# Casting a head's keys and queries in two halves, with another draw of the instruction order and 151 moves behind it

## The chip, the cores and the metric

The kernel runs on one core of one Trainium2 chip. The metric is the device time of one execution in microseconds, and each version is executed several times. The engines are TensorE (PE, with PEld for the loading of its weights), VectorE (DVE), ScalarE (ACT), GpSimd (POOL) and SyncE (SP), which here does nothing but issue transfers between DRAM and on-chip memory.

## The reference

One layer of a hybrid trunk is computed for 1024 prompt rows and 32 sample rows of width 1024. Cut to what matters:

```python
qA, kA, vA, gA, qB, kB, vB, gB = split(rmsnorm(h, g_pre) @ w_in)     # 1024 -> 8 x 512
oA = band_attention(qA, kA, vA)        # 8 heads of 64; softmax over the own 64-row chunk and the 8 before
oB = stick_breaking(qB, kB, vB)        # 8 heads of 64
y  = concat(oA * silu(gA), oB * silu(gB)) @ w_out                    # 1024 -> 1024
h  = h + rmsnorm(y, g_post)
h  = h + sigmoid(h @ w_ple_gate) * (p @ w_ple)                       # p: 256 per row

# stick_breaking: z = q k * scale, causal
log_beta = log_sigmoid(z);  log_1m = log_sigmoid(-z)
w = exp(log_beta + (cumsum of log_1m from the right, without the own one))
```

The sample rows attend to 512 cached rows as well as to their own. Beside `h` the kernel returns the new keys and values of both attentions.

## The kernel before, in words

All numbers are 32-bit floats. A float32 matrix is split into a high part, cast to the format that TensorE multiplies (`fp32r`), and a low part, the rest; a product is three matmuls: high by high, high by low, low by high. In names, `wh_` and `wl_` are the two parts of a weight block, `hnh` and `hnl` those of the normed rows, `wTh` and `wTl` those of the turned attention weights, `kd` and `kl` those of a head's keys, `L` both parts of a head's queries (the high one in one half of the partitions, the low one in the other).

The work is laid out in four pairs of heads, 0 to 3. For each pair the eight parts of the input projection are multiplied (`mm_qA`, `mm_kA`, ... `mm_gB`), and between these long rows of matmuls the attention of the pair's four heads (two of A, two of B) is strewn in. For a head, `prep_k` and `prep_q` (lines 679 to 695) cast keys and queries out of `st`, 64 partitions by 1024 columns: ScalarE makes the high part, GpSimd the low part of the keys, VectorE that of the queries; then two transfers copy `kd` and `kl` to the other 64 partitions. Then, by blocks of 128 rows, PE makes the scores (`SA`, `SB`), VectorE, ScalarE and GpSimd make weights of them (`om`, `be`), the weights are turned (small ones by PE as `ptwA`, `ptwB`; the last blocks of a head by VectorE and a way out to DRAM, `swapA<-om`, and back, `be<-swapA`), ScalarE casts the high part `wTh`, VectorE subtracts the low part `wTl`, and PE multiplies with the values (`PVA`, `PVB`). In `PVA30_1` the letter is the attention, the first digit the pair, the second the head in it, and the number behind it the half of the rows. A head's result goes to DRAM (`o_dr<-otA`). The sample rows do the same on the pair's data (`SsA`, `SsB`, queries `QsA`, `QsB`). At the start the per-layer input `pp` is turned by PE (`ptp`) and multiplied with `w_ple` (`ple`, weights `wph`, `wpl`). At the end stand the output projection and the gate projection over blocks of 512 (`o0P` to `o3P`, `g0P` to `g3P`; each by seven products of sums of blocks, the sums `oB`, `gB` made by GpSimd and kept in `sum_dro`, `sum_drg`).

No engine call is issued where it is written. A `Recorder` takes each as an `Op` with the ops it must come after; `emit` (line 489) issues them at the end in the order that `order` (line 382) returns, so every instruction of the profile has the one line L502. `plan` (line 424) is a list scheduler: it runs a clock per engine with a cost table of its own and always takes the ready op with the smallest key. `order` runs `plan` once, and then `PASSES` times: `due` (line 399) walks back over the last order and sets each op's key to its latest time; a random number of spread 400 ns is added to the keys of everything that isn't PE; `plan` runs again. The random numbers come from a generator with a fixed seed, so the order is always the same one. An engine executes its instructions in this order; SyncE issues transfers in it.

Of the kernel before, what the change touches and what calls it, by code (L numbers as in the profile page):

```python
# [12 lines left out]
ALU = mybir.AluOpType  # L13
# [3 lines left out]
SEQ = 1024  # L17
# [21 lines left out]
BEHIND = 2  # L39
RATE = 1.0  # L40
PLE_LAG = 4.0
PASSES, SPREAD = 42, 400


def f(ap):

    return ap.bitcast(F32)
# [219 lines left out]
class Recorder:  # L267
# [113 lines left out]
    def order(self):  # L381

        for place, old in self.turns:
            place.after.update(x[0] for x in old.uses)
        users = {id(o): [] for o in self.ops}
        for o in self.ops:
            for a in o.after:
                users[id(a)].append(o)
        spread = random.Random(22)
        best, end = self.plan(users)  # L390
        for _ in range(PASSES):
            self.due(best, users, end)
            for o in self.ops:
                if o.eng not in ("CTL", "PE"):
                    o.key = (o.key[0] + spread.gauss(0, SPREAD), o.key[1])
            best, end = self.plan(users)
        return best

    def due(self, out, users, end):

# [107 lines left out]
def stream_step(  # L508
# [7 lines left out]
    nc = rec  # L516
# [66 lines left out]
    def load_w(j):  # L583

        if j >= len(order) or j in raws:
            return
        kind, p = order[j]
        c0 = NAMES.index(kind) * 512 + p * P
        raws[j] = []
        for kh in range(2):  # L590
            raw = wpool.tile([P, 4, P], F32, tag="wr", name=f"wr_{kind}{p}_{kh}", bufs=4)
            dma(raw, w_in[0, kh * 512:(kh + 1) * 512, c0:c0 + P].rearrange("(k p) c -> p k c", p=P))
            raws[j].append(raw)

    def ensure(j):

        if j >= len(order) or j in loaded:
            return
        load_w(j)
        kind, p = order[j]  # L600
        loaded[j] = []
        if j == 2:
            pair = [ringl.tile([P, 2, 4, P], f"w{x}_{kind}{p}") for x in "hl"]
        for kh in range(2):
            raw = raws[j][kh]
            if j == 2:
                hi, lo = (x[:, kh] for x in pair)
            else:
                hi = wpool.tile([P, 4, P], F32R, tag="wh", name=f"wh_{kind}{p}_{kh}", bufs=4)
                lo = wpool.tile([P, 4, P], F32R, tag="wl", name=f"wl_{kind}{p}_{kh}", bufs=4)  # L610
            (nc.gpsimd.tensor_copy if j < 3 else nc.scalar.copy)(hi, raw)
            nc.gpsimd.tensor_tensor(lo, raw, f(hi), ALU.subtract)
            loaded[j].append((hi, lo))
# [12 lines left out]
    HALF = [slice(0, 512), slice(512, 1024)]  # L626
# [50 lines left out]
    def halves(h):  # L677
        return slice(h * HD, (h + 1) * HD), slice((1 - h) * HD, (2 - h) * HD)

    def prep_k(nm, h, st):  # L680
        r, o = halves(h)
        kd = opnd[h].tile([P, SEQ], F32R, tag=f"kd{h}", name=f"kd{nm}{h}")
        kl = opnd[h].tile([P, SEQ], F32R, tag=f"kl{h}", name=f"kl{nm}{h}")
        nc.scalar.copy(kd[r], st[r, 0:SEQ])
        nc.gpsimd.tensor_tensor(kl[r], st[r, 0:SEQ], f(kd[r]), ALU.subtract)
        dma(f(kd[o]), f(kd[r]))
        dma(f(kl[o]), f(kl[r]))
        KDh[h], KLD[h] = kd, kl

    def prep_q(nm, h, st):  # L690
        r, o = halves(h)
        L = opnd[h].tile([P, SEQ], F32R, tag=f"L{h}", name=f"L{nm}{h}")
        nc.scalar.copy(L[r], st[r, 0:SEQ])
        nc.vector.tensor_tensor(L[o], st[r, 0:SEQ], f(L[r]), ALU.subtract)
        Lq[h] = L

    def prep_v(nm, h, tok):
# [552 lines left out]
    for n in range(-1, 8):  # L1250
        a = len(order)
        if n < 7:
            ab, p = pairs[n + 1]
            order += [(k + ab, p) for k in "kqv"]
        for _ in range(share.get(n, 0)):
            order.append(gates.pop(0))
        span.append((a, len(order)))
# [3 lines left out]
    for n, (ab, p) in enumerate(pairs):  # L1261
        for h in range(2):
            for k, fn in (("k", prep_k), ("q", prep_q), ("v", prep_v)):
                prep[n, h, k] = lambda ab=ab, p=p, h=h, k=k, fn=fn: fn(f"{ab}{p}", h, src_of[k, ab, p])
# [209 lines left out]
    L, R = HALF  # L1474
# [307 lines left out]
    for m, (nm, src, group) in enumerate(sets):  # L1782
        last_set = m == len(sets) - 1
        state = [{}, {}]
        for n, prod in enumerate(ORDER):
            for pair, t in enumerate(group):
                st = state[pair]
# [150 lines left out]
```

## Time and profile before

| what | value |
|---|---|
| median of 3 runs | 774.38 us (772.48 to 774.99) |
| profiled execution | 774.27 us, of which the span of the trace is 772.5 us |
| instructions in the trace | 13671 |
| PE matmuls | 4422, busy 759.3 us |
| PE idle in the span | 13.2 us |
| bytes moved by transfers | 182.24 MB, 236 GB/s on average |

The trace is of one execution. Its span runs from the first to the last instruction; 1.8 us of the execution lie outside. Engine names and tile names are those above, with their numbers left out, so that all heads of one kind share a group. "Busy" of PE is the time in which at least one matmul was in flight; the end of a matmul is modelled. "Idle" beside an instruction is the time in which its engine did nothing just before it, with what ended it. For SyncE, the length of a row is the time that it took to issue the transfer, and not the time the transfer took.

### The profile page before, as it was taken

The page shows a single profiled execution, that of the slowest core. Times are in us where ns is not written, and L with a number is a line of the kernel's source. Part 1 is how long each engine was busy: PE and PEld are TensorE (multiplying, and loading weights), DVE is VectorE, ACT ScalarE, POOL GpSimd, SP SyncE. Part 2 cuts the span into 40 slices and gives each one's busy share as a digit, 9 for nine tenths or more (in the row PEclk, how much of TensorE's full clock was granted, in tenths as well). Part 3 has the DMA queues.
Part 4 walks back from the last instruction along what each step waited for, and adds up shares of the span by engine and source line. Part 5 has one row for each costly group of instructions (what it writes and reads, how often), then busy time and mean ns, then how long its engine had stood idle before and what let it go on. Part 6 is the DMA issues. An engine that isn't in the chain of part 4 may idle for free.

```text
span 772.5 us, 13671 instructions
## 1 busy us (share of the span) xinstructions
PE 759.3 (98%) x4422; PEld 700.0 (91%) x4422; DVE 588.9 (76%) x1025; ACT 489.7 (63%) x995; POOL 462.5 (60%) x525
## 2 busy tenths in 40 slices
PE   8999999999999999999999999999999999999997
PEld 6999999999999999999999899999998877888786
DVE  6816789898799888988998698775473578587675
ACT  6636686667685657875567695633357967774551
POOL 6614628794354546656782346787453769899443
PEclk9999999999999999999999999999999999999999
DMA  8519999788986649999678679966688859879854
GB/s 278 168 40 292 263 293 286 224 248 247 236 231 199 158 148 292 262 288 280 186 242 259 170 209 279 292 205 205 190 286 254 282 150 339 277 253 324 284 183 137
DMA packets 184825, 182.24 MB, mean 236 GB/s; under 512 B 42177, under 2 KB 139497, under 8 KB 184754
## 3 DMA queue, kind: packets, MB, share of 16 engines
q1 hardware_dynamic: 184754, 181.37, 77.7%
q8 instruction: 35, 0.57, 0.3%
q14 instruction: 36, 0.29, 0.1%
HBM read 107.62 MB, written 65.30 MB: 224 GB/s over the span
## 4 chain that ended last, share of the span: by engine, by line
PE 72%; DMA 12%; ACT 4%; DVE 4%; SPq 3%; POOL 3%; issue 2%; ACTq 0%; POOLq 0%; DVEq 0%
PE mm_gB L502 6%; PE mm_kA L502 5%; PE mm_vA L502 5%; PE mm_qA L502 4%; PE mm_gA L502 4%; PE mm_qB L502 3%; PE mm_vB L502 3%; PE PVB L502 3%; PE SB L502 3%; SPq L502 3%; PE g1P L502 3%; PE o3P L502 3%; PE o1P L502 3%; PE g0P L502 2%; PE o0P L502 2%; PE o2P L502 2%
## 5 line engine op out<-in xcount | busy, mean ns | idle before, releaser
L502 POOL TENSOR_TENSOR be<-om 128x128 f32<-128x128 f32 (+7 forms) x64 | 79.4, 1247 | 50.5 <-DVE om L502 17.1
L502 DVE TENSOR_TENSOR_SCAN om<-om,SB 128x384 f32<-128x384 f32 (+5 forms) x96 | 94.2, 998 | 7.5 <-ACT om L502 4.2
L502 DVE TENSOR_TENSOR wTl<-be,wTh 128x640 fp32r<-128x640 f32 (+2 forms) x56 | 64.6, 1158 | 13.6 <-ACT wTh L502 13.5
L502 ACT ACTIVATE om<-SB 128x384 f32<-128x384 f32 (+5 forms) x96 | 44.7, 491 | 26.5 <-PE SB L502 11.3
L502 ACT CAST wTh<-be 128x640 fp32r<-128x640 f32 (+2 forms) x56 | 43.3, 776 | 23.8 <-DMA be<-swapA 12.6
L502 ACT ACTIVATE be<-om,statA 128x640 f32<-128x640 f32 (+3 forms) x64 | 46.4, 730 | 15.7 <-DVE statA L502 7.5
L502 DVE STREAM_TRANSPOSE om<-be 128x640 f32<-128x640 f32 (+2 forms) x56 | 49.3, 890 | 2.9 <-ACT be L502 1.8
L502 POOL TENSOR_TENSOR gB<-gB,gB 128x256 f32<-128x256 f32 x32 | 26.5, 846 | 17.4 <-DMA gB<-in_w_ple_gate_dram 8.2
L502 DVE CUSTOM_DVE_ANT_0 om<-SA,biasA 128x320 f32<-128x320 f32 (+3 forms) x64 | 29.7, 483 | 7.2 <-PE SA L502 6.1
L502 POOL TENSOR_TENSOR oB<-oB,oB 128x256 f32<-128x256 f32 x32 | 27.0, 868 | 10.9 <-DMA oB<-in_w_out_dram 9.5
L502 PE MATMUL SB<-klB,LB 128*128 128x384 f32 (+5 forms) x96 | 32.9, 347 | 0.0
L502 PE MATMUL SB<-kdB,LB 128*128 128x384 f32 (+5 forms) x96 | 32.5, 344 | 0.3 <-DVE om L502 0.3
L502 ACT CAST wTh<-ptwB 128x512 fp32r<-128x512 f32 (+3 forms) x48 | 22.0, 482 | 17.0 <-PE ptwB L502 11.2
L502 POOL TENSOR_TENSOR sggA<-sggA,oggA 128x352 f32<-128x352 f32 x24 | 25.4, 1061 | 8.1 <-DVE sggA L502 5.5
L502 DVE TENSOR_TENSOR wTl<-ptwB,wTh 128x512 fp32r<-128x512 f32 (+3 forms) x48 | 25.4, 542 | 5.8 <-PE PVB L502 3.6
L502 PE MATMUL SA<-klA,LA 128*128 128x320 f32 (+2 forms) x96 | 29.4, 318 | 0.0
L502 PE MATMUL SA<-kdA,LA 128*128 128x320 f32 (+2 forms) x96 | 29.3, 316 | 0.0
L502 POOL TENSOR_TENSOR klB<-stkB,kdB 64x1024 fp32r<-64x1024 f32 x8 | 19.2, 2402 | 12.2 <-ACT kdB L502 10.0
L502 DVE TENSOR_TENSOR SB<-SB,maskb 128x128 f32<-128x128 f32 x64 | 17.4, 286 | 10.4 <-PE SB L502 10.3
L502 POOL TENSOR_TENSOR klA<-stkA,kdA 64x1024 fp32r<-64x1024 f32 x8 | 19.5, 2438 | 8.2 <-DMA ple_dr<-pleo 6.3
L502 POOL TENSOR_TENSOR h<-h,x 128x512 f32<-128x512 f32 (+1 forms) x18 | 23.2, 1299 | 1.5 <-DVE h L502 1.4
L502 PE MATMUL ptwB<-ident,be 128*128 128x128 f32 x144 | 21.8, 274 | 0.9 <-POOL be L502 0.7
(683 smaller groups left out, 2584.6 us busy)
## 6 DMA issues: line engine op xcount, KB each, us to landing
swapA<-om SPq DMA_DIRECT2D x32, 320.0 KB
be<-swapA SPq DMA_DIRECT2D x32, 320.0 KB
oB<-in_w_out_dram SPq DMA_DIRECT2D x16, 256.0 KB
sum_dro<-oB SPq DMA_DIRECT2D x16, 256.0 KB
gB<-in_w_ple_gate_dram SPq DMA_DIRECT2D x16, 256.0 KB
sum_drg<-gB SPq DMA_DIRECT2D x16, 256.0 KB
x<-in_x_prompt_dram SPq DMA_DIRECT2D x16, 256.0 KB
turned<-hs SPq DMA_DIRECT2D x16, 256.0 KB
```

Of the source, the lines that this page charges most:

```text
L502: getattr(getattr(tc.nc, o.what[0]), o.what[1])(*args, **kw)
```

## The change

It has three parts. The casts of a head's keys and queries, and the two subtractions, are made for columns 0 to 511 and then for 512 to 1023, each half in instructions of its own; the transfers that copy `kd` and `kl` stay whole and come behind both halves. The number of passes goes from 42 to 19 and the seed from 22 to 31, so that the order is another one. And behind the last pass `settle` takes 151 pairs (i, j) one after the other: it takes the op at index i of the list (9477 entries) to index j, a few places ahead, together with those between that it needs. Of the moved ops 54 are on SyncE, 47 on VectorE, 19 on ScalarE, 17 on PE and 14 on GpSimd; most pass one to three instructions of their engine.

```diff
+MOVES = (
+    (9138, 9132), (2784, 2777), (4231, 4180), (214, 200), (7520, 7500), (7547, 7536), (199, 189), (3210, 3202), (4808, 4790), (9117, 9104), (1473, 1409),
...
+    (428, 420),
+)
-PASSES, SPREAD = 42, 400
+PASSES, SPREAD = 19, 400
...
-        spread = random.Random(22)
+        spread = random.Random(31)
...
-        return best
+        return self.settle(best)
+
+    @staticmethod
+    def settle(ops):
+
+        for i, j in MOVES:
+            x = ops[i]
+            need, engines, ahead, behind = set(x.after), {x.eng}, [], []
+            for o in reversed(ops[j:i]):
+                if o in need or (o.eng in engines and o.eng != x.eng):
+                    assert o.eng != x.eng
+                    ahead.append(o)
+                    need |= o.after
+                    if o.eng != "CTL":
+                        engines.add(o.eng)
+                else:
+                    behind.append(o)
+            ops[j:i + 1] = ahead[::-1] + [x] + behind[::-1]
+        return ops
...
     def prep_k(nm, h, st):
...
-        nc.scalar.copy(kd[r], st[r, 0:SEQ])
-        nc.gpsimd.tensor_tensor(kl[r], st[r, 0:SEQ], f(kd[r]), ALU.subtract)
+        for c in HALF:
+            nc.scalar.copy(kd[r, c], st[r, c])
+            nc.gpsimd.tensor_tensor(kl[r, c], st[r, c], f(kd[r, c]), ALU.subtract)
         dma(f(kd[o]), f(kd[r]))
         dma(f(kl[o]), f(kl[r]))
...
     def prep_q(nm, h, st):
...
-        nc.scalar.copy(L[r], st[r, 0:SEQ])
-        nc.vector.tensor_tensor(L[o], st[r, 0:SEQ], f(L[r]), ALU.subtract)
+        for c in HALF:
+            nc.scalar.copy(L[r, c], st[r, c])
+            nc.vector.tensor_tensor(L[o, c], st[r, c], f(L[r, c]), ALU.subtract)
```

PE's instructions stay 4422 and SyncE's transfers 734; ScalarE has 32 more, VectorE and GpSimd 16 more each. Three places of the new order are shown, each of before and then of after.

GpSimd at the start of the program: `wph0`, `wpl0` are the parts of the first 128 rows of `w_ple`, `wph1` the high part of the next; `ms` are the mean squares of the norm. Before:

```order
L502 CAST wph0True_190<-wpr0_1True_198 128x512
L502 TENSOR_TENSOR wpl0True_191<-wpr0_1True_198,wph0True_190 128x512
L502 TENSOR_SCALAR ms1_213<-ms1_213 128x1
L502 TENSOR_TENSOR ms1_213<-ms1_213,halfp_180 128x1
L502 CAST wph1True_192<-wpr1_1True_199 128x512
```

After:

```order
L539 CAST wph0True_190<-wpr0_1True_198 128x512
L539 TENSOR_SCALAR ms1_213<-ms1_213 128x1
L539 TENSOR_TENSOR ms1_213<-ms1_213,halfp_180 128x1
L539 CAST wph1True_192<-wpr1_1True_199 128x512
L539 TENSOR_TENSOR wpl0True_191<-wpr0_1True_198,wph0True_190 128x512
```

The subtraction `wpl0` has moved behind the cast `wph1`.

GpSimd at the first head of B: `be<-om` are the weights that PE turns next (`ptwB`), `wl_kA1` low parts of the second pair's key weights, `oB210` a sum of blocks of the output weights, whose operand comes by a transfer. Before:

```order
L502 TENSOR_TENSOR wl_kA1_0_1306<-wr_kA1_0_884,wh_kA1_0_1336 128x512
L502 TENSOR_TENSOR wl_kA1_1_1317<-wr_kA1_1_910,wh_kA1_1_1342 128x512
L502 MEMSET om_197 128x1
L502 TENSOR_TENSOR oB210_1386<-oB110_995,oB210_1386 128x256
L502 TENSOR_TENSOR be_211<-om_197 128x128
L502 TENSOR_TENSOR oB210_1386<-oB110_995,oB210_1386 128x256
```

After:

```order
L539 TENSOR_TENSOR klB01_1256<-stkB0_1047,kdB01_1253 64x512 x2
L539 MEMSET om_197 128x1 x3
L539 TENSOR_SCALAR qsS_183<-stqB0_1084 128x32
L539 TENSOR_TENSOR be_211<-om_197 128x128
L539 TENSOR_TENSOR be_211<-om_197 128x256
L539 TENSOR_TENSOR wl_kA1_0_1338<-wr_kA1_0_876,wh_kA1_0_1363 128x512
```

The first weights stand ahead of the low parts `wl_kA1` and of the sum `oB210`, and behind the halves of the next head's keys.

SyncE at the first band head of the fourth pair: `swapA30_7<-om` and `be<-swapA30_7` take the weights of its last block out and back; `kdB30` is the copy of the keys of the pair's next head, `out_4<-ktB3` stores of new keys, `sum_drg` a sum of gate weights, `vnsA1` rows of the samples. Before:

```order
L502 DMA swapA30_7_150<-om_197 128x640
L502 DMA be_211<-swapA30_6_149 128x4x160
L502 DMA be_211<-in_cache_a_v_dram 128x4x256
L502 DMA kdB30_5185<-kdB30_5185 64x1024
L502 DMA out_4_dram<-ktB3_5235 32x32x32 x2
L502 DMA be_211<-swapA30_7_150 128x4x160
L502 DMA out_4_dram<-ktB3_5235 32x32x32 x2
```

After:

```order
L539 DMA swapA30_7_150<-om_197 128x640
L539 DMA o_dr3_66<-otA30_0_5111 64x512
L539 DMA be_211<-swapA30_6_149 128x4x160
L539 DMA be_211<-in_cache_a_v_dram 128x4x256
L539 DMA be_211<-swapA30_7_150 128x4x160
L539 DMA kdB30_5254<-kdB30_5254 64x1024
```

The load of the last block has moved ahead of the key copy and of the two stores, and the transfer of the first half's result, `o_dr3<-otA30_0`, has moved behind the way out.

13 rows, old and new, of the table MOVES are left out of this document.

## The prediction

> **What bounds the kernel now.** I read the page's engine shares first, then the busy time in two stretches, then TensorE's waits, then the chain of work that ended last, and at last the single places that the waits name.
>
> The engine shares and the DMA line of the page:
>
> ```profile
> span 772.5 us, 13671 instructions
> PE 759.3 (98%) x4422; PEld 700.0 (91%) x4422; DVE 588.9 (76%) x1025; ACT 489.7 (63%) x995; POOL 462.5 (60%) x525
> PEclk9999999999999999999999999999999999999999
> ```
>
> TensorE (PE) is busy 759.3 of 772.5 us at full clock in every slice, and nothing else is above 76%. 13.2 us is idle PE. That, and not the 775, is what another order can touch. The page named "Perfetto Trace Analysis" of the Trainium skill, section "Identifying the Most-Contended Engine", objects that matmul busy is no good measure of closeness to the limit and that the weight-load share should be read instead; by PEld's 91% some 72 us would be open, so that a new order might give far more than I forecast. The rows of the chain below speak against it: 214 matmuls stand there in one piece, with no wait named among them; I give it no chance.
>
> The waits of TensorE, summed by what was waited for (us in total, times, longest):
>
> ```profile
> PE idle L502 <- DVE still L502: 1.3, 1, 1.3
> PE SsA L502 <- ACT QsA L502: 1.3, 1, 1.3
> PE ptp L502 <- DMA pp<-in_p_prompt_dram: 1.1, 1, 1.1
> PE SsB L502 <- ACT QsB L502: 0.8, 1, 0.8
> PE PVA L502 <- ACT wTh L502: 0.8, 1, 0.8
> PE ptwB L502 <- POOL be L502: 0.7, 1, 0.7
> PE PVB L502 <- DVE wTl L502: 0.6, 1, 0.6
> PE ple L502 <- POOL wph1True L502: 0.6, 1, 0.6
> PE SB L502 <- DVE om L502: 0.3, 1, 0.3
> PE ptwB L502 <- POOL sumsA L502: 0.2, 1, 0.2
> ```
>
> These sum to 7.7 us, in ten places, each once. The first 1.3 is the wait for the first constant and can't go; 6.4 us can. The chain shows the rest of the idle time, and what one matmul is worth:
>
> ```profile
> 420.04 6.22 DMA o_dr<-otA
> 548.55 34.60 PE mm_gB L502 x214
> 765.69 1.46 PE g3P3b L502 x12
> L502 PE MATMUL mm_gB<-hnh,wh_gB 128*128 128x352 f32 x96 | 18.2, 326 | 0.0
> ```
>
> (The first three rows: start, length, what; the last is from the groups.) The last matmul ends at 765.69 + 1.46 = 767.15, so 772.5 − 767.15 = 5.4 us is a tail without PE, on the other engines; 7.7 + 5.4 is the 13.2 within rounding. A matmul in an unbroken row costs 34.60/214 = 0.162 us, while its own record is 0.326 long: its end lies 0.164 us after the next could have begun. So I count a wait at its shown gap and 0.164 more: behind a gap the next matmul begins only after that end. With all nine gone: 6.4 + 9 × 0.164 = 7.9 us, and the profiled execution, 774.27 us (span 772.5 and 1.8 around it), would come to 766.4. I make the sum against 774.27; the median of the three runs is 774.38, the same within 0.02%.
>
> The order of the last 1015 matmuls, from inside the first block of the gate projection B of the last pair (about 552 us before) to the end, is the same in both kernels, and so are the last twenty rows of every other engine. No wait of the list lies there. What the change does to PE must happen before about 550 us, and the tail stays.
>
> **The change part by part.** It (1) casts keys and queries in two halves, (2) draws another order of everything outside that last stretch, and (3) moves 151 instructions by a few places. (2) and (3) can't be told apart in the order, so I take their result, place by place.
>
> *The start: ptp and ple.* The new order issues both first loads of the prompt's per-layer input ahead of a weight load, and on GpSimd the cast wph1True stands ahead of the subtraction wpl0True:
>
> ```profile
> 5.78 0.66 PE L502 MATMUL ptp<-ident,pp 128*128 128x128 f32 x4 [1.10 <-DMA pp<-in_p_prompt_dram]
> 11.70 1.29 POOL L502 TENSOR_TENSOR wpl0True<-wpr_1True,wph0True 128x512 fp32r<-128x512 f32 x1
> 13.91 0.61 POOL L502 CAST wph1True<-wpr_1True 128x512 fp32r<-128x512 f32 x1
> 14.59 0.70 PE L502 MATMUL ple<-wph0True,php 128*128 128x512 f32 x2 [0.56 <-POOL wph1True L502]
> ```
>
> The cast comes 1.29 us earlier, more than the gap of 0.56, so that gap goes with its restart, 0.72. One issue less ahead of the second load is worth some 0.5 of the 1.10. Together 1.2; but this early PE waits for whatever loads, and time won at ptp is partly waited for again at the next weight. I take −0.7; ends 0 and −1.9.
>
> *Halves.* 32 casts on ScalarE, 16 subtractions on VectorE and 16 on GpSimd become two each. The groups by form:
>
> ```profile
> L502 ACT CAST kdB<-stkB 64x1024 fp32r<-64x1024 f32 x8 | 8.4, 1047 | 0.5 <-PE SA L502 0.3
> L502 ACT COPY otB<-PVB 64x512 f32<-64x512 f32 x16 | 9.3, 582 | 8.7 <-PE PVB L502 8.4
> L502 ACT CAST wh_kB<-wr_kB 128x512 fp32r<-128x512 f32 x8 | 5.0, 619 | 3.2 <-PE mm_kA L502 2.8 <-PE mm_qA L502 0.4
> L502 DVE TENSOR_TENSOR LB<-stqB,LB 64x1024 fp32r<-64x1024 f32 x8 | 11.1, 1388 | 0.7 <-ACT LB L502 0.5
> L502 DVE TENSOR_TENSOR v2A<-vtA,v2A 128x512 fp32r<-128x512 f32 x8 | 5.4, 680 | 0.0
> L502 POOL TENSOR_TENSOR klB<-stkB,kdB 64x1024 fp32r<-64x1024 f32 x8 | 19.2, 2402 | 12.2 <-ACT kdB L502 10.0 <-DVE wlsA L502 1.4 <-POOL om L502 0.8
> ```
>
> ScalarE: two of 582 less 1047 is 0.12 us, two of 619 less 1047 is 0.19; by 32, 3.7 to 6.1 us. VectorE: two of 680 against 1388, nothing. GpSimd: by the 512-wide subtraction wpl0True of 1.29 us above, 2 × 1.29 less 2.40 is 0.2, by 16 it is 3 us. All of it lies on engines that are idle 37%, 24% and 40% of the span, and no PE wait names a key or query operand; what hides it is the projection matmuls of the next pair. If that cover is gone at one head, it costs 0.12 to 0.2 there. What halves can give is a shorter hold of an engine (0.6 instead of 1.05 us on ScalarE) to a waiting cast. The two key copies by DMA still wait for both halves. I put 0 on the path; ends −1 and +1 us. The Trainium skill ("Perfetto Trace Analysis", section "Optimizing Scalar/DVE Operations") speaks against splitting with a fixed cost of about 93 ns on ScalarE and 60 ns on VectorE per instruction, which as an estimate gives 3.0 and 1.0 us, and a sum of 775.3 if both engines were on the path; the VectorE rows above don't show its 60 ns, and the same section allows breaking work up on an engine that isn't saturated.
>
> *The first head of B (ptwB, 0.7).* On GpSimd a subtraction that waits for a load of output weights stands ahead of the mask that PE transposes; in the new order it stands behind:
>
> ```profile
> 109.36 0.73 POOL L502 TENSOR_TENSOR oB<-oB,oB 128x256 f32<-128x256 f32 x1 [2.76 <-DMA oB<-in_w_out_dram]
> 110.05 0.39 POOL L502 TENSOR_TENSOR be<-om 128x128 f32<-128x128 f32 x1
> ```
>
> GpSimd was idle 2.76 us before the subtraction, so 0.73 and much of 2.76 goes from the front of the mask, and the cover on PE grows from 45 to 49 matmuls. The gap of 0.73 goes: −0.89 with its restart. End: 0, if VectorE's part ahead of the mask is late by as much.
>
> *Second pair, band head 0 (PVA, 0.8).* SyncE issues the transfers; ScalarE's cast waits for the second load of the swapped weights:
>
> ```profile
> 194.89 2.05 SPq L502 DMA_DIRECT2D kdB<-kdB  x1
> 196.98 1.49 SPq L502 DMA_DIRECT2D out_dram<-ktB  x2
> 198.59 1.15 SPq L502 DMA_DIRECT2D be<-swapA  x1
> 199.78 0.74 SPq L502 DMA_DIRECT2D out_dram<-ktB  x1
> 200.56 0.47 SPq L502 DMA_DIRECT2D be<-swapA  x1
> 206.04 0.72 ACT L502 CAST wTh<-be 128x640 fp32r<-128x640 f32 x1 [1.96 <-DMA be<-swapA]
> ```
>
> In the new order the key copy kdB still stands ahead of both loads, the three stores of ktB behind: 1.49 + 0.74 = 2.2 us less ahead of the last load, and two matmuls more cover. The wait of 0.78 goes: −0.94. What is now ahead instead (a 32-row load and a block of output weights) costs two issues; end 0.
>
> *Third pair, B head 0 (PVB, 0.6, and small ones).* Cover 134 to 138 matmuls: 4 × 0.162 = −0.65. The small waits at SB and ptwB (0.3 and 0.2) have some matmuls more of cover: −0.3. Ends 0 and −1.3.
>
> *The samples (SsA 1.3, SsB 0.8).* SsA keeps 46 matmuls and the same transfer of 6.22 us behind it: 0. SsB loses 7 matmuls of cover, 1.1 us, but its query's cast moves ahead of two casts of ScalarE, and the transfer ahead of it is issued before a 512 KB store: 0; ends +1.1 and −0.96 (the wait and its restart).
>
> *Fourth pair, band head 0 (PVA, no wait before).* The order shows 162 matmuls from the last scores to the second value product before, 135 now: 27 × 0.162 = 4.4 us less cover. The rows there:
>
> ```profile
> 427.04 0.51 SPq L502 DMA_DIRECT2D kdB<-kdB  x1
> 427.65 1.54 SPq L502 DMA_DIRECT2D out_dram<-ktB  x2
> 429.30 2.82 SPq L502 DMA_DIRECT2D be<-swapA  x1
> 435.16 0.73 ACT L502 CAST wTh<-be 128x640 fp32r<-128x640 f32 x1 [0.63 <-DMA be<-swapA]
> 435.95 0.85 PE L502 MATMUL PVA<-wTh,v2A 128*128 128x512 f32 x4
> ```
>
> The last cast ends at 435.89 and PE takes it at 435.95: nothing is in hand. In the new order the last load stands ahead of kdB and ktB: 0.51 + 1.54 = 2.05 us at least; and its issue, 2.82 here against 0.47 for its like above, may shrink by 2.35, which makes 4.4. So the wait there lies between 0 and 4.4 − 2.05 = 2.35, and 4.4 with its restart 4.6 if the queue gives nothing. Since a store's issue ahead of it is what the slow issue follows in both places, I take it nearest to the low end: +0.5.
>
> The sum: −0.7 − 0.89 − 0.94 − 0.65 − 0.3 + 0 + 0.5 = −2.98. 774.27 − 2.98 = 771.3 us.
>
> **The rivals.**
> *Slower: the fourth pair's cover.* The chain from scores to weights (ScalarE, VectorE, swap out and back, cast) takes as long as before, PE comes 4.4 us sooner and waits them. For it: 0.06 us in hand, and the new halves and copies share the queue. Against it: the rows of the queue above. Then +4.6 there, +1.1 at SsB, and of the gains those that the cover alone gives (start 0.7, ptwB 0.65, PVB 0.65, small 0.3): +5.7 − 2.3 = +3.4, 777.7 us. With SsB's 1.1 it turns the sum against the change once more than 1.2 us of wait stand there.
> *Half of it.* The queue gives just the 2.05: wait 2.35, with its restart 2.5 instead of 0.5, so 773.3; with SsB's 1.1, 774.4: no change to measure.
> *It does nothing.* A new draw closes waits and opens others of the same size, since places like the last one above have 0.06 us in hand and any of them can turn into a wait: 774.3.
> *All waits go.* SsA and SsB too, and no new ones: 766.4, the floor worked out above. Against it: 46 matmuls of cover at SsA in both orders.
>
> **How the numbers follow.** Forecast 0.5 with its own range 769.5 to 772; slower 0.2; half 0.14; nothing 0.1; all waits 0.06. What this kernel's measurement can tell from no change is about 0.3%, 2.3 us. Faster by more (below 772.0): 0.5 + 0.06 and a little of the half case, 0.57; within: 0.22; slower: 0.21. The range takes the floor's end and the slower case in: 766.5 to 778.0.
>
> **What would show it.** In the profile after: no PE wait for wph1True; none for a mask be at the first B head; none for wTh at the second pair; SsA's 1.3 still there; the fourth pair's PVA with under 1 us for wTh, which is the step I trust least. PE busy should stay at 759 us, idle PE fall to about 10.5, the tail stay 5.4, and ScalarE's busy time rise by 4 to 6 us. The forecast is wrong if a new wait above 2 us stands anywhere in PE's list, or if the last stretch no longer starts about 3 us sooner and runs its same length.

## The result: 0.6% slower, where a gain was forecast

The changed kernel takes 778.57 us (median of 6 runs, 775.32 to 783.02) against 773.74 of the kernel before beside it (6 runs, 771.73 to 777.95): a ratio of 1.0060, with a 95% interval of 1.0031 to 1.0088. The forecast was 771.3, in a range of 766.5 to 778.0: it has the wrong sign, and the time lies 0.57 us above the range.

The profiled execution of the changed kernel took 783.02 us, the slowest of the six. Its page (span and engine shares):

```profile
span 781.2 us, 13761 instructions
PE 764.5 (98%) x4422; PEld 703.8 (90%) x4422; DVE 590.8 (76%) x1041; ACT 507.9 (65%) x1039; POOL 466.7 (60%) x541
```

TensorE is still the bound, busy 98%, with the same 4422 matmuls, but for 5.2 us more than before. ScalarE is busy 18.2 us more, where 4 to 6 were expected. The list of TensorE's waits (us in total, times, longest):

```profile
PE PVB L539 <- DVE v2B L539: 4.5, 2, 2.4
PE ple L539 <- ACT wph0True L539: 1.4, 1, 1.4
PE idle L539 <- DVE still L539: 1.3, 1, 1.3
PE ptwB L539 <- POOL om L539: 1.1, 2, 0.8
PE PVA L539 <- ACT wTh L539: 0.8, 2, 0.6
PE SA L539 <- DVE statA L539: 0.7, 1, 0.7
PE ptwB L539 <- POOL be L539: 0.6, 1, 0.6
PE ptwA L539 <- DVE wTl L539: 0.5, 2, 0.3
PE ptksA L539 <- DMA be<-in_cache_a_k_dram: 0.2, 1, 0.2
PE SB L539 <- DVE LB L539: 0.2, 1, 0.2
PE PVA L539 <- DVE wTl L539: 0.2, 1, 0.2
```

The two waits for the samples' queries (SsA, SsB), that for wph1 and that for the prompt input are gone, and so are the two waits that the prediction placed at the second pair's first band head (PVA) and at the first mask of the first B head (rows of the same names stand at other places now). New are two waits for `v2B`, the low part of the values of a B head, 2.1 and 2.4 us. The chain of work that ended last, its long piece near the end and its last matmuls (start, length, what):

```profile
559.10 33.19 PE mm_gB L539 x205
774.88 1.46 PE g3P3b L539 x12
```

The last matmul ends at 776.34, 9.2 us later than before, and 4.9 us of tail follow (5.4 before). Of the 9.2, the wait list carries 11.5 − 7.7 = 3.8; five more gaps at the prediction's 0.164 each carry 0.8.

At most 1.7 us more are lost to the clock. Behind the first wait for `v2B` TensorE ran at half rate. The busy time per slice of 1 us (PE, PEld, DVE, ACT, POOL, then the granted clock, the DMA share and GB/s):

```profile
140.00:141.00 1.00, 1.00 (x5) 0.95 (x6) 1.00 (x2) 0.32 (x1) 1.00 (x4) 0.78 1.12 353
141.00:142.00 1.00, 1.00 (x5) 0.90 (x4) 1.00 (x2) 0.40 (x1) 1.00 (x2) 0.50 1.15 365
142.00:143.00 1.00, 1.00 (x4) 0.85 (x4) 0.50 (x3) 0.84 (x2) 1.00 (x1) 0.50 1.17 402
143.00:144.00 1.00, 1.00 (x6) 0.98 (x5) 1.00 (x2) 1.00 (x3) 0.10 (x1) 0.51 0.95 192
```

0.22 + 0.50 + 0.50 + 0.49 = 1.7, which PE counts as busy. That leaves 2.9 us of the 9.2 without a row. They are hardly idle time: PE is idle for 781.2 − 764.5 = 16.7 us, and the list and the tail make up 11.5 + 4.9 = 16.4 of it. So most of them must lie where a matmul starts late while the one before it still counts as in flight. The two places of `v2B`, from the timeline of the changed kernel (start, length, engine, what; in brackets the idle time before and what ended it):

```profile
136.15 1.29 POOL L539 TENSOR_TENSOR klA<-stkA,kdA 64x512 fp32r<-64x512 f32 x1 [2.89 <-ACT kdA L539]
136.62 3.22 DVE L539 TENSOR_TENSOR v2B<-vtB,v2B 128x512 fp32r<-128x512 f32 x1 [0.36 <-ACT v2B L539]
137.41 1.88 POOL L539 TENSOR_TENSOR be<-om 128x1024 f32<-128x1024 f32 x1
139.99 0.93 PE L539 MATMUL PVB<-wTh,v2B 128*128 128x512 f32 x4 [2.13 <-DVE v2B L539]
...
376.66 0.82 PE L539 MATMUL PVB<-wTh,v2B 128*128 128x512 f32 x4 [2.42 <-DVE v2B L539]
```

VectorE's subtraction of 128x512, 0.68 us in the prediction's rows, takes 3.22 here. It began while GpSimd made a half of the keys (`klA`), was passed by GpSimd's next instruction, and ended 0.55 us after that one (137.41 + 1.88 = 139.29; 136.62 + 3.22 = 139.84).

### The profile page after: what moved, and what is told of

Read it like the earlier page. It is cut to its first block, busy times and chain, and to the rows that moved or that the text cites. A ratio compares the mean times of both kernels' runs of the same rounds, so it can differ in the third digit from the quotient of the medians.

```text
span 781.2 us, 13761 instructions
## 1 busy us (share of the span) xinstructions
PE 764.5 (98%) x4422; PEld 703.8 (90%) x4422; DVE 590.8 (76%) x1041; ACT 507.9 (65%) x1039; POOL 466.7 (60%) x541
## 4 chain that ended last, share of the span: by engine, by line
PE 74%; DMA 11%; DVE 5%; ACT 4%; SPq 3%; issue 2%; POOL 0%; DVEq 0%; ACTq 0%
PE mm_gB L539 6%; PE mm_qA L539 6%; PE mm_gA L539 6%; PE mm_vA L539 5%; DMA be<-swapA 4%; PE mm_kB L539 4%; PE PVB L539 4%; PE ple L539 3%; SPq L539 3%; PE mm_kA L539 3%; PE g1P L539 3%; PE o3P L539 3%; PE o1P L539 3%; PE mm_qB L539 2%; PE g2P L539 2%; PE g0P L539 2%
## 5 line engine op out<-in xcount | busy, mean ns | idle before, releaser
L539 POOL TENSOR_TENSOR be<-om 128x896 f32<-128x896 f32 (+7 forms) x64 | 82.3, 1292 | 55.2 <-DVE om L539 25.0
L539 DVE TENSOR_TENSOR wTl<-be,wTh 128x640 fp32r<-128x640 f32 (+2 forms) x56 | 56.4, 1016 | 6.1 <-ACT wTh L539 5.9
L539 ACT ACTIVATE be<-om,statA 128x640 f32<-128x640 f32 (+2 forms) x64 | 46.5, 731 | 11.3 <-DVE statA L539 5.6
L539 POOL TENSOR_TENSOR klB<-stkB,kdB 64x512 fp32r<-64x512 f32 x16 | 22.8, 1431 | 22.2 <-ACT kdB L539 22.1
L539 POOL TENSOR_TENSOR oB<-oB,oB 128x256 f32<-128x256 f32 x32 | 25.0, 802 | 15.5 <-DMA oB<-in_w_out_dram 13.3
L539 DVE CUSTOM_DVE_ANT_0 om<-SA,biasA 128x320 f32<-128x320 f32 (+4 forms) x64 | 29.8, 484 | 5.8 <-PE SA L539 3.6
L539 POOL TENSOR_TENSOR klA<-stkA,kdA 64x512 fp32r<-64x512 f32 x16 | 20.6, 1295 | 21.6 <-ACT kdA L539 14.5
L539 PE MATMUL PVB<-wTh,v2B 128*128 128x512 f32 (+1 forms) x96 | 21.0, 341 | 4.5 <-DVE v2B L539 4.5
```

The costliest lines, as they stand in the source:

```text
L539: getattr(getattr(tc.nc, o.what[0]), o.what[1])(*args, **kw)
```

## The experiments

The kernel before was run beside each group of experiments, on the same chip; its median was 772.97 to 773.47 in the five groups. Ratios are to it, with 95% intervals.

### Taking the change apart

The first question was which part costs, and whether the two new waits are the cause. The rival was that a draw of the order is a draw, good or bad, whatever waits it shows. Four kernels.

Without the 151 moves:

```diff
-        return self.settle(best)
+        return best
```

> The changed kernel without the 151 moves behind its last pass. My theory (the values' chain: the low part v2B of the values of the first B head of pairs 0 and 2 comes late, because of the new draw and the halves): no row of that chain is touched by a move, so the two waits of TensorE for v2B stay, 2.0 to 2.5 us each, and the time is 777 to 783 us, equal to the changed kernel's 778.6 or a little above it, since some small waits come back. Rival (the moves did the harm): both waits for v2B are gone or under 0.5 us, and the time is 774 or less.

779.79 us, 1.0095 (1.0060 to 1.0130). The moves don't do the harm. A repeat beside the unchanged pair (below) gave 1.0071 against 1.0055 of the changed kernel, with intervals that overlap: the moves gain 0 to 3 us, and no run settles how much.

The halves alone, in the order of before: each of the four instructions is issued as two, one right behind the other.

```diff
         nc.vector.tensor_tensor(L[o], st[r, 0:SEQ], f(L[r]), ALU.subtract)
+        rec.ops[-1].parts = [(L[o, c], st[r, c], f(L[r, c]), ALU.subtract) for c in HALF]
```

(and likewise for the two casts and for `kl`)

> The kernel before, its order untouched, only that each of the four casts and subtractions of a head's keys and queries is issued as two halves, one right behind the other. My theory: halves by themselves cost engine time (ScalarE busy 4 to 6 us more) and nothing on the path; the time is within 1 us of the kernel before, 773 to 775 us, and no wait for v2B above 0.5 us. Rival (the extra instructions are what makes the change slower): 776 us or more, with new waits behind ScalarE or GpSimd.

777.64 us, 1.0065 (1.0045 to 1.0084): the halves, which the prediction put at 0, cost 4.7 us in the order of before.

The keys whole again, in the changed order, at the place of their second half:

```diff
-        for c in HALF:
-            nc.scalar.copy(kd[r, c], st[r, c])
-            nc.gpsimd.tensor_tensor(kl[r, c], st[r, c], f(kd[r, c]), ALU.subtract)
+        # first half: nothing; second half: the whole of kd and kl
```

> The changed kernel, its order untouched, only that the high and low part of a head's keys are again made in one instruction each, at the place of the second half; queries stay in halves. At the first B head of pair 0 the first half of klA then no longer stands on GpSimd between the value casts and the weights be, and its cast no longer ahead of the cast of v2B on ScalarE. My theory: VectorE's subtraction v2B there falls from 3.22 us to under 1.5 us and the wait there from 2.1 to under 1 us; the wait at pair 2 (2.4 us), where no half of klA stands between, stays; the time falls by 1 to 4 us against the changed kernel, to 775 to 778 us. Rival (only the place of the chain in the order counts, GpSimd does not hold VectorE): the wait of 2.1 us stays within 0.5 us.

779.72 us, 1.0096 (1.0063 to 1.0129). Not faster, so it isn't the halves of the keys that hold the changed order up.

The two waits for `v2B` closed, by moves on ScalarE and GpSimd in the changed order:

```diff
+    ("ACT", "v2B00<-vtB0", 0, "kdA10<-stkA1", 0),
+    ("ACT", "v2B01<-vtB0", 0, "kdA10<-stkA1", 0),
+    ("POOL", "beB00_7<-omB00_7", 0, "klA10<-stkA1", 0),
+    ("POOL", "wl_vA3_0<-wr_vA3_0", 0, "beB20_7<-omB20_7", 0),
```

(the op named first is taken ahead of the second)

> The changed kernel with four instructions moved, no transfer and no matmul: in pair 0 ScalarE makes both value casts v2B ahead of the first half of kdA, and GpSimd makes the weights be (1024 columns) ahead of the first half of klA; in pair 2 GpSimd makes a low weight part (wl_vA) ahead of the weights be (1024 columns), so that neither stands in front of VectorE's subtraction of v2B when it starts. My theory (GpSimd's instruction holds VectorE's two-operand subtraction until it is done): the subtraction takes 0.65 to 0.7 us in both places instead of 3.22 and 1.92, TensorE's waits for v2B fall from 4.5 us together to under 1.3 us, and the time to 774 to 776 us. Rival (the chain is late because its transfers are late): the waits stay above 3.5 us together.

777.72 us, 1.0059 (1.0037 to 1.0081). The waits closed and the time stayed (the changed kernel itself, run again below, takes 777.67): 0.2 us is left at `v2B`, while the mask of B costs more (two rows of its TensorE waits):

```profile
PE ptwB L578 <- POOL om L578: 2.2, 3, 1.4
...
PE PVB L578 <- DVE v2B L578: 0.2, 1, 0.2
```

So the largest two waits of the profile were not what made the kernel slower. My theory of that moment fell here.

### Which half costs, and what a draw is worth

One engine's halves at a time, in the order of before, and the new draw alone, with whole casts.

```diff
+        rec.ops[-1].parts = [...]     # on VectorE's L only / ScalarE's kd and L only / GpSimd's kl only
```

```diff
-PASSES, SPREAD = 42, 400
+PASSES, SPREAD = 19, 400
-        spread = random.Random(22)
+        spread = random.Random(31)
```

> The kernel before in its own order; of the four instructions only VectorE's subtraction of the queries (L) is issued as two halves. My theory after the run with all four in halves (777.6 us against 773.0 in the same session, VectorE busy 8 us more, its subtraction of the queries 19.0 and 15.7 us in all instead of 12.9 and 11.1): each half of a two-operand subtraction has to wait for GpSimd's running instruction anew, and VectorE's delay reaches TensorE by the maxima of the scores (statA). VectorE busy rises by 4 to 8 us, and 2 to 4 of the 4.7 us show here: 775 to 777 us. Rival (ScalarE's added instructions carry the loss): under 1 us, 772.5 to 774 us.

> The kernel before in its own order; only ScalarE's casts of keys and queries are issued as two halves. My theory (VectorE and GpSimd carry the loss): ScalarE busy 5 us more and less than 1 us on the path, 772.5 to 774 us. Rival (ScalarE's 32 added instructions carry it): 3 us or more, 776 us and above.

> The kernel before in its own order; only GpSimd's subtraction of the keys (kl) is issued as two halves. My theory: GpSimd busy 3 to 5 us more; between its two halves a waiting VectorE instruction gets in, which helps VectorE and delays GpSimd, so the sum is small: 772.5 to 775 us. Rival (GpSimd carries the loss): 776 us and above.

> The kernel before with whole casts, 19 passes and seed 31: another draw, without halves and moves. My theory (the halves carry the loss and a draw by itself is worth a few us either way): 771 to 778 us, with three to twelve waits of TensorE of under 2.5 us. Rival (any other draw of this kind loses what the draw before was chosen for): 777 us and above, as much as the changed kernel.

| kernel | median, us | ratio |
|---|---|---|
| VectorE's halves | 777.65 | 1.0061 (1.0039 to 1.0083) |
| ScalarE's halves | 773.17 | 0.9998 (0.9983 to 1.0013) |
| GpSimd's halves | 774.30 | 1.0014 (0.9995 to 1.0032) |
| the draw alone | 777.58 | 1.0062 (1.0038 to 1.0085) |

The cost of the halves shows with VectorE's alone, whose term the prediction put at nothing. For ScalarE's 32 and GpSimd's 16 more instructions, also put at nothing on the path, no time could be measured; the intervals leave them at most 0.13% and 0.32%. The page of VectorE's halves, then its subtractions of A's queries by tile, in the kernel before and here (lowest, median and highest of one in ns, first and last start):

```profile
PE 759.3 (98%) x4422; PEld 700.4 (90%) x4422; DVE 597.0 (77%) x1041; ACT 488.2 (63%) x995; POOL 460.4 (59%) x525
```

```profile
L502 DVE TENSOR_TENSOR LA<-stqA,LA x8: 1220/1500/2365, 60.9 to 398.9; 64x1024 fp32r<-64x1024 f32 x8
```

```profile
L503 DVE TENSOR_TENSOR LA<-stqA,LA x16: 675/1244/2377, 60.9 to 402.0; 64x512 fp32r<-64x512 f32 x16
```

Undisturbed, a half takes 0.68 and a whole 1.22: 0.14 more by the pair, 2.2 us in 16. But VectorE is busy 8.1 us more. The rest is halves that take up to 2.4 us, twice a whole. One place of it, from the timeline of VectorE's halves:

```profile
295.52 1.30 POOL L503 TENSOR_TENSOR wl_qB<-wr_qB,wh_qB 128x512 fp32r<-128x512 f32 x1 [1.78 <-DMA kdA<-kdA]
...
296.07 3.60 DVE L503 TENSOR_TENSOR LA<-stqA,LA 64x512 fp32r<-64x512 f32 x2
...
296.79 2.34 POOL L503 TENSOR_TENSOR be<-om 128x1024 f32<-128x1024 f32 x1
```

The two halves together end at 299.67, and GpSimd's `be` at 299.13: 0.54 us before. Taken one by one, the first half ends 0.55 us after `wl_qB` and the second 0.55 us after `be`. Every lengthened subtraction of queries in the traces of this kernel and of the kernel before ends that 0.55 us (a half) or 1.08 us (a whole) after the end of a GpSimd instruction: it stands still until that is done, and makes nearly all of its work then. In the kernel before 6 of the 16 wholes were caught so, for 4.5 us above the lowest; of the 32 halves 13, for 12.5 us. About four in ten are caught either way: with twice as many instructions, the second half can be caught behind the next GpSimd instruction after the first half got through. The Trainium skill ("SBUF — State Buffer", section "Who interferes with whom") says that a VectorE instruction with two SBUF inputs contends with a GpSimd instruction that reads SBUF, and calls the lock on the ports that they share exclusive; the fixed 0.55 and 1.08 us behind the end of GpSimd's instruction agree.

How these 8 us become 4.5 us of time is seen in part. TensorE now waits for A's softmax, which VectorE makes (the first two rows of VectorE's halves):

```profile
PE SA L503 <- DVE statA L503: 2.2, 3, 1.1
PE SA L503 <- DVE om L503: 1.7, 1, 1.7
```

Neither row stood in the list before. That the block, and not the mere 2.2 us of overhead, makes the time isn't shown: no run took the block away. With GpSimd's halves VectorE's whole subtractions took 27.7 us instead of 24.0, and no time could be measured.

In the changed order this added time is mostly absent. The same 32 halves in its profile:

```profile
L539 DVE TENSOR_TENSOR LA<-stqA,LA 64x512 fp32r<-64x512 f32 x16 | 14.9, 933 | 8.3 <-ACT LA L539 7.8
L539 DVE TENSOR_TENSOR LB<-stqB,LB 64x512 fp32r<-64x512 f32 x16 | 13.0, 814 | 1.4 <-ACT LB L539 1.0
```

They take 27.9 us there, against 24.0 for the wholes of the kernel before and 33.0 for the halves in its order, and VectorE is busy 1.9 us more than before, not 8.1. So the 4.5 us can't be carried over to the changed kernel.

The draw alone costs 4.4 us, with whole casts: about as much as the whole change. Draw and halves, 4.4 and 4.5, don't add up to the 4 to 5 us of the whole.

### Closing the waits that the prediction named

If the prediction's mechanism was right and only the draw spoiled it, closing its waits in the order of before must bring 2.5 to 3.5 us.

```diff
+    ("POOL", "wph1True<-wpr1_1True", 0, "wpl0True<-wpr0_1True", 0),
+    ("POOL", "beB00_0<-omB00_0", 0, "oB210<-oB110", 0),
+    ("SP", "beA10_7<-swapA10_7", 0, "ktB1", 2),
+    ("SP", "beA10_6<-swapA10_6", 0, "ktB1", 2),
+    ("SP", "o_dr7<-otB30_0", 0, "vtB3", 0),
+    ("ACT", "QsB1<-QfsB1", 0, "wThB30_1<-ptwB30_7_0", 0),
```

> The kernel before, whole casts and its own order, with six instructions moved so that the waits that my prediction wanted closed are closed there and nothing else changes: the cast wph1 ahead of the subtraction wpl0, the first weights be of B ahead of the sum oB210, the two loads of swapA10 behind the key copy and ahead of the stores of ktB1, and for the samples of pair 3 the transfer of otB30 ahead of the store of vtB3 and the query cast QsB1 ahead of two weight casts. By the prediction's own terms: -0.72 - 0.89 - 0.94 and up to -0.96 for SsB, so 2.5 to 3.5 us less than the kernel before, 769.5 to 771 against 773. If only their sizes in one profile were read and a typical execution has less: -0.5 to -2 us. Rival (such waits come back elsewhere within the same pair): within 0.5 us of before.

774.85 us, 1.0009 (0.9994 to 1.0023): nothing. The places closed, and others stand in the list, which sums to 8.4 us, against 7.7 before. Its first row:

```profile
PE ptx L543 <- DVE hnl L543: 1.8, 1, 1.8
```

The same was tried on the changed order: the four moves above, two loads of `stvB2` ahead of two stores, and a load of `w_ple` ahead of the second load of `pp`.

```diff
+    ("SP", "stvB2<-swapB2", 0, "vxB2", 0),
+    ("SP", "stvB2<-swapB2", 1, "vxB2", 0),
+    ("SP", "wpr0_0True", 0, "pp0", 1),
```

> The changed kernel with the new waits of its profile taken out by moves: the four instructions at the two places of v2B as before, the loads of stvB2 ahead of two small stores, and the first weight of the per-layer product issued ahead of the second input load again. If the changed kernel is slower by those waits (4.5 for v2B, 1.35 for wph0, with the half-rate stretches behind them 1.7 and 1.8): 772 to 775 us. Rival (they are what one execution happened to show, and the loss is spread over the whole order): 776.5 us or more.

777.24 us, 1.0042 (1.0027 to 1.0057): at most a little of the loss comes back. Two more draws came with it, without the 151 moves: the halves with 42 passes and seed 22, and whole casts with 42 passes and seed 31.

```diff
-PASSES, SPREAD = 19, 400
+PASSES, SPREAD = 42, 400
-        spread = random.Random(31)
+        spread = random.Random(22)
```

> Halves as in the changed kernel, but the draw with the numbers of the kernel before (42 passes, seed 22), no moves; the operations are other ones, so the order is a third one. If a draw by itself is worth a few us either way and the kernel before has a good one: 776 to 782 us, like the draw of the changed kernel without its moves (779.8). Rival (seed 31 with 19 passes is a bad draw): 773 to 775 us.

> Whole casts, 42 passes as before, seed 31: one more draw without halves and moves. If the kernel before has a good draw among many: 775 to 780 us. Rival (the number of passes matters, 42 gives better orders than 19): 772 to 774 us.

782.85 us, 1.0115 (1.0094 to 1.0135), and 782.68 us, 1.0133 (1.0111 to 1.0155). With the draw alone and the kernel without moves, these are four other draws, two of them with halves, and each is 4 to 10 us slower than the kernel before. Its order is better than any of these four, so a new draw starts from a loss here; more draws weren't run.

### How far one profile speaks for its kernel

Both kernels were run again unchanged, and the one without moves.

> The kernel before, unchanged, for a second profiled execution. If a wait of TensorE under 1.5 us is a property of the order, the list shows the same places with the same sizes within 0.3 us (SsA 1.3, ptp 1.1, SsB 0.8, PVA 0.8, ptwB 0.7, PVB 0.6, ple 0.6). If it is what one execution happened to show, half of these places are gone or differ by more than 0.5 us, others stand in the list, and the sum is again 6 to 9 us.

> The changed kernel, unchanged, for a second profiled execution and more times, in the same session as its version without moves. If the waits for v2B (2.1 and 2.4 us) belong to the order, both are there again within 0.5 us; if they are one execution's, one or both are under 1 us and other waits stand in the list. Time 777 to 779.5 us either way.

> The changed kernel without its 151 moves, beside the changed kernel on the same chip. If the moves give back part of what the draw loses: 1 to 3 us slower than the changed kernel, 779 to 781 us. Rival (the moves do nothing that can be measured): within 1 us of it.

774.02 us, 1.0001 (0.9984 to 1.0018); 777.67 us, 1.0055 (1.0033 to 1.0077); 780.24 us, 1.0071 (1.0046 to 1.0096). The second profile of the kernel before, first rows of TensorE's waits:

```profile
PE ptwB L502 <- POOL be L502: 2.3, 2, 1.4
PE idle L502 <- DVE still L502: 1.3, 1, 1.3
PE ptp L502 <- DMA pp<-in_p_prompt_dram: 1.3, 1, 1.3
PE PVA L502 <- ACT wTh L502: 0.8, 2, 0.4
```

Of the seven waits named, three are there again within 0.2 us: ptp, the first mask of the first B head (0.89, at 111.35 us; the other 1.42 of its row is a mask of the third pair, at 343.67), and PVB. Two have shrunk (the second pair's 0.78 to 0.34, SsB's 0.83 to 0.25), and two are gone: the one for wph1, and SsA's 1.3, the largest that any work could close. The sum is 7.3 us again. So neither expectation holds whole: part of the list belongs to the order, and part to one execution. The second profile of the changed kernel, first rows:

```profile
PE idle L539 <- DVE still L539: 1.3, 1, 1.3
PE ple L539 <- ACT wph0True L539: 1.3, 1, 1.3
```

The wait for wph0 is there again. There is no row for `v2B`: the subtraction took 0.67 and 1.14 us at the two places, and the values were 0.86 and 0.93 us early. This execution took 774.21 us, as long as the first profiled one of the kernel before; others of the same kernel took up to 782.32. By the program's order and the times of the traces, TensorE takes an operand that another engine has just made at 406 places, and at 98 and 92 of them, in the two profiles of before, the operand had been ready for less than 1 us. Which of these are late changes in part from one execution to the next; a list of waits is in part a sample.

### ScalarE's table loads

The 18.2 us of ScalarE were still unexplained. The group of table loads, before and after:

```profile
L502 ACT ACT_TABLE_LOAD x10 | 12.8, 1283 | 0.9 <-PEq L1926 0.7
```

```profile
L539 ACT ACT_TABLE_LOAD x22 | 28.2, 1283 | 1.1 <-PEq L1965 0.7
```

12 more loads of 1.28 us are 15.4 of the 18.2. One place of the changed kernel, ScalarE around 102 us:

```profile
102.17 1.28 ACT L539 ACT_TABLE_LOAD   x1
103.47 0.28 ACT L539 ACTIVATE om<-SB 128x128 f32<-128x128 f32 x1
...
106.60 1.28 ACT L539 ACT_TABLE_LOAD   x1
107.90 0.90 ACT L539 ACTIVATE be<-om,statA 128x640 f32<-128x640 f32 x1
```

The exponentials of A's softmax (`be<-om,statA`) and the sigmoids of B (`om<-SB`) need different tables. By the order, with halved queries B's first scores can be made earlier (35, 47, 42 and 35 matmuls behind the last of the queries' projection before; 10, 26 and 15 ahead of it now in three pairs and 1 behind in one), so B's first sigmoids fall between A's last exponentials. Two ways to price it: 12 loads put into the kernel before, by six one-column exponentials between sigmoids, whose results the next sigmoid overwrites; and 6 taken out of the changed kernel, by four activations moved on ScalarE, alone and with the moves above.

```diff
+                if o.eng == "ACT" and ... in EXTRA:
+                    tc.nc.scalar.activation(args[0][:, 0:1], self.halfp.get()[:, 0:1], AF.Exp)
```

```diff
+LATER = (
+    ('omB30_1<-SB30_1_0', 'beA31_7<-omA31_7'),
+    ('omB30_0<-SB30_0_0', 'beA31_7<-omA31_7'),
+    ('beA11_7<-omA11_7', 'beA11_6<-omA11_6'),
+    ('beA21_7<-omA21_7', 'beA21_6<-omA21_6'),
+)
```

(the op named first waits for the second: the sigmoids come behind it, the exponentials to just ahead of it)

> The kernel before in its own order, with six extra Exp of one column on ScalarE, each between two Sigmoids of the first rows of a head of B: twelve more loads of an activation table, 22 instead of 10, as many as the changed kernel has and at about its places (pair 0 one, pairs 1 and 2 two each, pair 3 one). Their column is overwritten by the next Sigmoid. If the twelve loads (1.28 us each, 15.4 us of ScalarE) are what the changed kernel pays for: 775 to 778 us against 773.4. Rival (ScalarE, idle over a third of the span, hides them): under 1 us, 773 to 774.5 us.

> The changed kernel with four activations of ScalarE moved: in pairs 1 and 2 the Exp of the last but one band block stands right ahead of the last one's, in pair 3 two Sigmoids stand behind one Exp; 16 loads of a table instead of 22, 7.7 us of ScalarE less. If the loads are what the changed kernel pays for: 1.5 to 3 us less than its 777.7, 775 to 776 us. Rival (hidden, or the later Exp costs as much): within 1 us, 776.7 to 778.7 us.

> The changed kernel with all of the moves so far: the four at v2B, the loads of stvB2, the first weight of the per-layer product (together 777.2 us) and the four activations (16 table loads). The best version of the changed order that I have. If table loads and named waits add up: 773 to 775.5 us. Rival (the loss is spread over the order): 776 us or more.

Put in: 782.42 us, 1.0113 (1.0076 to 1.0149), 9.2 us for 12 loads, or 0.77 us for each (with half an exponential of one column). The place where it falls is plain, at B's masks:

```profile
PE SB L507 <- DVE om L507: 5.4, 4, 1.7
```

Taken out: 781.94 us, 1.0104 (1.0074 to 1.0133), and with the other moves 782.06 us, 1.0116 (1.0070 to 1.0161). The loads fell from 22 to 16, and by the ratios (1.0104 against the changed kernel's 1.0055 and 1.0060) the kernel got some 3 to 4 us slower (the intervals just touch): what was moved came late instead (first rows of TensorE's waits with the loads out):

```profile
PE PVsA L607 <- DVE newlsA L607: 1.8, 1, 1.8
PE SB L607 <- DVE om L607: 1.7, 1, 1.7
```

So a table load in the way of a head's chain costs; whether it does at the changed kernel's twelve places isn't shown, since taking six of them out moved the chain too. The draw alone has 10 loads, as the kernel before, and is 4.4 us slower nevertheless, and the two slowest draws have 14, eight fewer than the changed kernel: loads aren't the whole cause either.

No version here beats the kernel before.

## Why the prediction was wrong

*What bounds the kernel.* Right: TensorE at 98%, and only its gaps to win or lose. Wrong was the next step, the sum itself. It takes the listed gaps off the time at their full length, and puts everything else that the new draw does at nothing. The −2.98 is made of closings (0.7, 0.89, 0.94, 0.65 and 0.3) less 0.5. Its main places did what the prediction said: in both profiles of the changed kernel wph1, the first mask of the first B head and the second pair's first band head show no wait. It was worth nothing all the same. These three and SsB's wait, closed by themselves in the order of before, were to bring 2.5 to 3.5 us and brought none (1.0009, at best 0.06% less). And the new draw by itself, with whole casts, cost 4.4 us. These are the two steps that failed: a closing counted at its gap, and the rest of the draw at nothing. Why a closing brings nothing is in part argued: TensorE comes earlier to some ninety other places with less than 1 us in hand, and waits there; but the moves can also have made other instructions late, and no run tells the two apart.

*The start, −0.7.* The wait for wph1 went, and one for wph0 came, 1.4 and 1.3 us in the two profiles; the prediction had the end 0 for it, "time won at ptp is partly waited for again at the next weight".

*Halves, 0 with ends −1 and +1.* Mis-sized: 4.7 us in the order of before, though not shown for the changed order, where VectorE is busy 1.9 us more. The term for VectorE, "two of 680 against 1388, nothing", took the mean of eight wholes, which holds the caught ones, against a half from undisturbed rows. Lowest against lowest it is 2 × 0.68 against 1.22, and caught against caught far more. ScalarE's and GpSimd's terms were right: nothing on the path that could be measured.

*ScalarE, 4 to 6 us more.* 18.2, as the 12 table loads were not counted. The order of the instructions names no table loads, but it shows exponentials and sigmoids, and each change from one to the other can be counted in it.

*The samples.* "SsA's 1.3 still there": it isn't, and in the second profile of the kernel before it isn't either.

*Fourth pair, +0.5.* No wait at band head 0 in either profile. The cover fell by more than was counted: from the end of the last scores to the product it is 26.2 us in the trace before and 20.1 in that of the changed kernel, 6.1 less where 4.4 were forecast. But the chain from the scores to the last cast took some 7 us less: 4.0 between the way out and the cast, where the prediction had counted 2.05 as certain, and 3.0 ahead of the way out, where the exponential came sooner. The last cast of the weights and its product, from the timeline of the changed kernel; the cast was 0.90 us early (440.27 + 0.73 = 441.00, and PE comes at 441.90):

```profile
440.27 0.73 ACT L539 CAST wTh<-be 128x640 fp32r<-128x640 f32 x1 [1.44 <-DMA be<-swapA]
...
441.90 0.73 PE L539 MATMUL PVA<-wTh,v2A 128*128 128x512 f32 x4
```

*The rivals.* The slower one has the right sign and nearly the size (777.7 against 778.57), by a mechanism that didn't happen: the fourth pair's band head 0 waits for nothing. That its number comes near is luck. "It does nothing", with its places that have 0.06 us in hand, names what defeated the sum, but expected new waits only of the size of the old ones. What it lacked is that the order of before is better than a draw is likely to be: four others, with or without halves, cost 4 to 10 us.

*What the cause is.* Shown: VectorE's halves cost 4.5 us in the order of before; the new draw with whole casts costs 4.4; 12 table loads put into the order of before cost 9.2; the effects don't add, since the whole change costs 4 to 5 us. The changed order has the 12 loads, and little of VectorE's added time. Not settled: how much each carries in the changed order, where neither whole keys, nor closed waits, nor fewer loads made it clearly faster. That the draw carries most of it is likely, as it costs 4.4 us with 10 loads and whole casts, but not shown: VectorE's queries whole in the changed order were not tried.

## What to carry to other kernels

Where one engine is 98% busy, the few waits of one profile stand among a hundred near misses: profile the kernel twice before a wait goes into a sum, and don't take its full gap for the gain. Where the order is a good one already, price a new draw as a loss (here 0.6 to 1.3%) until a run says otherwise. Cost a split on VectorE by the lowest duration of each shape, and look beside it for GpSimd instructions that hold it: splitting doubles the times it can be caught, and the order decides how often it is. When activations of two kinds change their order, count the table loads.

## What the runs showed of the hardware

In the changed kernel's first profile the granted clock fell to half from 140.56 to 143.97 us, for 3.413 us, behind an idle time of TensorE of 2.13 us; it stayed full behind one of 2.42 us at 376 us, in the same execution. The stretches of full clock ahead of the fall and behind it last 129.7 and 634.9 us, 38 and 186 times 3.413, so the clock changed on a grid of 3.413 us. In the interval of the grid that ended with the fall TensorE was busy for 1.28 us. The second idle time lies across a bound of the grid (376.08), with 1.58 us busy in the interval ahead of it and 2.83 in the one behind. The Trainium skill ("TensorE: Matmul & The Clock Gate", section "What's actually happening") lets the clock go down after an idle window of some 3.4 us that runs on its own. The grid agrees; but neither idle time was that long, so the window that slowed here held some work. How little work counts as idle isn't shown.

A VectorE subtraction of two operands that GpSimd holds up ends a fixed time after GpSimd's instruction, 0.55 us for 64x512 and 1.08 us for 64x1024, against 0.68 and 1.22 undisturbed: the wait replaces the instruction's start. One that has waited for one GpSimd instruction can be passed by the next that stands close behind it, and so a short instruction lasted 3.22 us instead of 0.68.
